# New order tables for four engines in a two-part encoder layer on one core

## The chip, the cores and the metric

The kernel runs on one core of a Trainium2 chip. A core has five engines that run side by side, each through its own list of instructions, strictly in the order of that list: TensorE (PE in the profile; its weight loads are shown apart as PEld), ScalarE (ACT), VectorE (DVE), GpSimd (POOL) and SyncE (SP), which issues the DMAs. An instruction starts when the one before it on its engine is out of the way and when the semaphores that it waits for have been raised by other engines or by DMAs. The metric is the device time of one execution in microseconds, the median of several runs.

## The reference, cut to what matters

One layer of an encoder for 1024 prompt rows and 64 sample rows, all in float32, model width 1024, hidden width 4096:

```python
z = x @ w_in                           # q,k,v of 6 FoX heads and 6 stick-breaking heads, u,v of the SGU
o_fox = softmax(q k^T/8 + c_t - c_s, causal) @ v      # c = cumsum(log f)
o_sb  = stick_breaking(q k^T/8, strictly causal) @ v  # one scan along the keys
o_sgu = gelu(u) * (tril(w_s) @ layer_norm(gelu(v)) + b_s)   # chunks of 128 rows
x1 = layer_norm(ALPHA * x + rms_norm_per_head(concat(o_fox, o_sgu, o_sb)) * g_mix @ w_out)
h  = square(relu(x1 @ w_up))
y  = layer_norm(ALPHA * x1 + h @ w_down)
```

The outputs are `y` for both groups of rows, and the new rows of keys, values, log gates and normalised `v`.

## The kernel before

**Products.** Every float32 operand of a large product is split in a high part, rounded to the type that PE reads (`hi`, written by ACT with a copy), and a low part (`lo = src - hi`, written by DVE or POOL in `lo_sub`, line 303). One product is three passes: high by high, high by low, low by high (`PASSES`). The two MLP products are done as seven block products in place of eight (Strassen's scheme in Winograd's form). PE has 8,827 matmuls.

**Stages.** The times are places in the span of the profile of before. (1) To about 520 us: the input projection (`kv_stage`, `q_stage`, `tok_mm`, line 583) is interleaved with the attention units (scores line 783, transposes line 831, values lines 841 to 844, softmax and stick-breaking rows on ACT, DVE and POOL). (2) 520 to 640 us: `mix`, the output projection (line 461) with its layer norm. (3) 640 to 990 us: the up product in 16 passes `p` of 256 hidden columns; each pass has two chains (`Chain`, s = 0 of 288 rows and s = 1 of 256 rows) of seven products (`product`, line 1536), written to the PSUM banks zA to zD. (4) 990 to 1332 us: the down product (`Down`, line 2001) into A, B and D. (5) After that the last rows' layer norm and their stores.

**The up stage, which the prediction follows in most detail.** For each pass `prep` loads two blocks of `w_up` (tile `wr`, line 1726). ACT and POOL split three blocks of them (tile `wa`, lines 1474 and 303). `w_sums` then forms four sums in place on DVE (lines 1483, 1484, 1486, 1487); ACT writes their high parts (tile `ws`, line 1757) and DVE their low parts (`ws`, line 303). A chain's results leave the banks by ACT (`sn<-zA`, line 1547) and DVE (lines 1550 to 1556). Then DVE does squared relu (line 1568) and four sums (lines 1577 to 1580) on tile `hh`, and SP stores them (lines 1581 to 1585). The first pass (p = 0) uses rows `y` and `h` of the mixer's pool in place of `hh`; the pool of all later passes lies in the same memory, so the first tiles of p = 1 must wait for what still reads the old rows.

**The order.** The Python code above is traced in one program order. After it, at the end of `_build` (lines 2356 to 2368), each engine's instructions are put in an order that is written out, by a planner, in the table `ORDER[engine]`. A table is a row of words `n+k`: take the instruction at place `k` of those that are left, n times (n is 1 and k is 0 where they are not written). Each instruction is made to follow the one taken before it. So a table is a permutation of the program order, and nothing else: it adds, removes and resizes no instruction. Given the permutation of before and the trace, in which the instructions stand in that order, each word of a new table names one instruction of the trace. The places, counts and distances "by the tables" in the prediction are read out in this way. Which buffer of a rotating pool a tile gets is decided by the build, after this order.

Of the kernel before, what the change touches and what calls it, by code (L numbers as in the profile page):

```python
# [50 lines left out]
+4 2 2+2 4 2+23 +25 4+23 12 4+12 2+32 +11 2+31 6 +5 +24 2+5 +51 2 +20 2+51 7+3 2+13 3 +39 +36 8 +10 2 +25 +51  # L51
2+25 6 +46 +2 4 +38 +40 2+14 +36 +65 2+36 +63 +14 4 +58 4 4+6 +79 1 +22 +48 5 +43 17 +53 +26 +52 +53 +82 3+52
2+26 +8 8 2+17 1 8+16 4 4+12 12 +10 18 7+2 +11 1 +10 +11 +10 8+1 1 +1 3 +24 4+27 3+24 32 8+2 1 +1 8 8+1 8+9
2+1 +3 2+6 +3 +1 +2 7+3 +1 8+2 +1 +8 38+1 8+3 2+5 +22 6+5 1 5+15 3 2+12 +14 1 +11 +12 14+11 3+54 +11 5+53
16+58 2+3 2+7 3 4+9 +4 2 4+10 2+2 4+14 2 +6 20+31 +18 1 3+5 1 3+13 +17 +21 +6 2 +14 2 +12 +2 3+13 +2 +10 3+2 2
+6 +5 3 4+7 1 +1 2 +13 1 +12 2+2 4+31 2 2+9 +8 8 +18 7+19 11+2 2+7 +17 +2 7+16 +24 3+2 +15 +2 1 +18 1 +12 +4
+21 +11 +14 2+12 +7 1 2+15 +20 6+9 +3 +5 1 4+11 +2 +5 1 +8 +1 1 2+6 7+12 2+6 +10 8+17 2+2 +19 +8 3+18 +4 +2
2+38 2+3 1 +35 +1 2+34 2+1 2+2 2 2+6 7+26 2+6 3+8 1 2+7 +30 +18 11+7 +25 1 +4 +39 +23 3+4 +13 +19 2+4 2+160
+11 +4 +10 2+31 2+4 3 2+1 1 +6 +146 4+19 +12 +18 +12 2 2+137 +10 3+136 5+138 +4 +137 2+4 +15 1 2+133 1 3+132
+2 +12 4+130 2 +10 +11 +10 +2 3+9 +121 9+122 3+2 2+12 4+2 4+8 +109 2+8 2 3+105 4+14 4 +2 2+96 +2 +8 +94 +2  # L60
3+35 +2 +6 +33 2+6 2+31 +6 2+2 3+4 5+2 +3 2+2 1 2+16 3+1 1 17+62 3+12 1 2+5 1 2+4 2+6 3+51 +6 3+50 2 +48 2+4
+46 2 +44 +2 2+45 4+6 6+2 2 2+36 2+2 2 2+1 2+22 1 2+31 2+6 1 +5 11+27 +5 1 +25 2 2+40 +75 2 2+38 +21 2+41 +21
1 2+66 2+39 6+20 +13 +23 +10 4+18 +12 +31 +17 1 5+47 +29 +46 1 +8 +27 +8 3 +23 2+30 3 +2 2+26 16+30 +13 +29
+13 2 4+26 2+50 6+26 +4 2+45 2+43 4 10+21 +6 4+28 2+2 2+18 +24 +7 +4 3+22 3+29 1 2+41 1 13+27 +4 +26 +13 2
3+26 +11 +25 +2 2+22 +68 5+21 6+31 +35 +31 1 +9 2 2+51 +27 1 +49 +6 2+30 1 +7 +25 1 2+26 +6 2+25 +6 2+22 4
2+30 +18 2+29 +35 +18 +2 +33 1 +8 +15 +1 +23 2+1 +24 +21 +1 +12 +4 +18 +20 +11 +4 +18 +9 +17 1 +3 +15 1 +6 +12
+11 2 +9 1 +3 +7 5+14 1 2+13 8+18 5+20 +88 +20 +87 +13 2+86 6+19 +23 2+19 3+2 2+3 2+2 +12 2+13 1 +11 1 3+10 4
+32 2 +2 8 2+13 6 +13 2+36 +19 +13 7 2+33 +6 2+32 2 +8 2+23 +10 1 +7 3 4+27 +21 +26 +4 1 +24 +19 1 +7 3+2 +14
+17 +48 2+6 +4 +5 +13 2+27 +10 +26 +4 3+38 +4 3+37 +4 +23 1 +8 +33 +13 1 2+19 +12 3+28 2+2 +10 +17 +15 +10 +14
+10 2+20 +10 +2 2+18 +19 2+18 +24 2+4 2+16 2+20 +9 +4 2+18 2+8 2+6 1 +5 2+8 +5 5+7 1 2+25 +4 +5 4+4 2+8 2+4  # L70
3+21 2+15 +6 +20 3+4 2+15 3+4 3+12 +4 2+7 3+11 2+7 1 2+3 1 +2 +4 2+8 8+40 16+42 +43 2 13+41 2+2 +4 2+38 +4 4+2
+4 1 6+1 1 3+6 4 2+2 2 19+13 2+10 8 5+3 5+20 +3 +6 +3 +17 +5 11+16 2+8 +2 2 9+9 2+2 1 +1 1 8+46 2+9 +15 +43
2+9 3+41 2+13 2+4 +49 +37 +11 3+36 +17 +4 3+16 4+39 1 2+38 3+30 2+22 1 8+27 +21 +8 +20 +44 2 +6 +41 +6 +40 +20
+9 +6 4+2 +33 1 +3 +12 +3 +11 1 10+10 2+17 4+2 2+7 3+6 2+2 3+37 8+6 3+13 2 +27 3+24 2+4 4+22 +4 2 4+6 3+15 +25
9+6 6+2 3+10 +38 1 2+15 2+9 2+13 +3 2+8 +1 +9 2+10 +1 +8 +14 2+1 2+6 1 2+23 1 +8 7+14 3+4 +7 +5 3+4 1 2+9 +7 1
+7 2+12 2+2 +4 +2 5+25 2+9 +23 6+2 +17 +5 2+3 8+2 +6 3+8 1 4+7 +16 3+7 1 +12 +67 2 2+4 1 +37 +61 1 +43 1 2+5
+58 +33 +55 1 +32 8 +24 +28 7 +21 +35 6 9+3 +37 +3 +6 +18 +6 +33 1 +4 1 +30 2+14 1 5+27 5+41 4+17 1 +5 +1 1 +3
1 2+11 2+40 +2 +28 2+10 6+36 +2 +35 +17 4+34 +24 +17 +32 1 +10 +1 +21 2+14 4+1 2+10 +20 2+10 2+1 +8 1 +14 4+22
3+2 +19 +4 2+10 +16 +4 +9 +4 +8 +4 +11 +7 +10 +7 +4 5+6 3+4 4+19 2+4 +6 +4 2+5 +4 +12 1 +11 1 2+10 6+2 +9 8+56
5+58 +2 3+57 +8 +3 +11 +7 1 +6 +8 +50 1 4+49 1 2+48 2+6 +46 +47 1 +9 3 5+42 +2 +5 10+40 2+5 3+2 2 +4 5 2+24 3  # L80
3+6 2 12+17 2+29 +17 +30 +42 +17 2+41 1 +28 5+16 +26 +3 1 +13 +23 2 5+11 5+22 1 3+21 4+19 2 11+17 1 2+58 +7 5
+2 3 +48 1 2+10 +16 2+10 1 +13 +4 2+12 22+37 +18 +28 2+4 3+16 +23 +10 2+22 7+26 +15 +25 +10 4 2+20 +39 2+20
+10 2+6 3+17 6 3+11 +22 +2 2+21 5+10 2+16 3+2 +7 +2 +6 +2 4+9 2 4+7 3+14 +7 4+13 2+22 +24 +25 2+24 1 +23 1 +11
1 +4 1 2+16 1 2+7 5+13 5+23 4+7 1 2+6 1 +9 +19 2+14 +17 1 +18 2 2+33 1 +15 2+13 6+29 2+35 +10 +12 1 +32 2 +5
4+29 +23 +28 +8 +5 3+7 3 +18 +7 1 +6 +12 1 +2 +20 +4 2+9 2+2 1 4+14 1 2+13 8+18 3+20 +13 +1 +4 4 +11 +12 +11
3+23 1 3+22 1 +21 2+1 4+19 3+7 1 9+6 1 4+5 1 8+4 4 2+1 +7 +1 +13 +6 8 +4 2+19 2+4 +17 2+18 +17 2+4 2 2+13 +65
8+27 3+41 +6 +40 2+2 2+4 +12 1 +11 1 +32 2+10 2+30 4+10 +26 3+34 4+18 8+30 1 3+29 +17 4+1 +13 1 2+12 +20 3+28
2 2+26 +4 4+17 2 3+19 1 +6 1 4+12 +5 2 +3 1 6+87 +2 4+25 2+82 4+25 2+88 8+80 +25 +2 +78 +24 +5 +12 3+2 2+5
3+17 4+2 2+63 2+3 +2 3+60 +61 1 3+60 3 10+57 +6 2+56 2 3+4 4 4+2 5 +1 2 7+35 +32 4 2+2 7+28 4 +34 +7 +21 +32
+7 4+21 +29 4+41 2+21 +7 +20 +7 +24 3+35 +19 1 2+18 2 2+29 2 2+19 +13 2+24 2 13+22 1 2+19 5 +5 3+55 4+18 +22  # L90
+6 +49 3+5 3 +15 +42 2+15 +6 2 4+37 2+4 16+35 4+16 +10 +30 2+22 2+28 2+22 4 4+22 3+26 +11 +25 +43 2+6 +9 1 +8
+38 6+20 1 +4 5+18 4 2+23 +14 +20 1 +19 7 8+12 6+19 1 2+18 +1 1 2+16 1 +2 5 6+9 8+15 2+23 +2 +22 +2 2 5+19
8+27 +5 1 2+7 2 3+2 1 8+25 6+31 2+11 2+29 4+36 +11 +5 1 +9 2 2+30 2 2+5 2+26 +5 2+3 14+27 2+10 4+25 +3 2+24 +3
3+27 2+10 +8 4+20 3 15+17 +5 2 3+20 2+14 1 2+17 +45 3+17 +2 5+72 5+12 +36 3+66 +80 2+38 4 +32 +73 2+32 1 +31 4
6+65 3+39 1 2+2 +7 2 2+5 2 3+29 1 2+3 +2 2 +4 +22 +4 2+21 +4 2 4+10 +2 2+9 3+2 3+8 2+6 +12 1 +11 +1 +24 +1 2+9
2+21 +1 1 5+19 2+7 1 6+16 2+6 +14 +15 +14 8+21 1 8+28 5+35 +3 2 +2 1 2+1 +9 2+6 +7 +6 +30 2+2 3+21 +1 2+3 1
7+21 4+34 3+60 1 9+33 +1 +49 2+32 +1 4+46 +31 +1 2+17 +42 2 2+15 1 2+37 4+18 5+33 +53 1 +2 1 +50 +1 1 4+48 +13
+9 3 +43 +9 +42 3 2+6 2+3 +4 +3 1 4+4 2 3+14 4+2 3+10 8 3+2 2 5+3 8+5 3+21 +3 2 2+1 2 2+14 2 3+12 8+27 3 3+3 3
+50 4+3 14+14 +4 +3 3 4+9 3 4+6 2+8 2 +6 7+4 7+5 +4 12+13 21+4 2 +2 +9 7+2 5+3 5+14 3+3 2+100 5+3 +2 2 4+3 26
2+18 +2 1 14+1 +44 +1 8 8+15 3+17 15 5+2 1 +3 1 2+5 7+11 3+9 16+10 +2 2+14 +49 1 2+13 10+46 1 +45 1 +6 2+14  # L100
2+22 +39 +5 +21 1 2+12 3+34 +4 +33 +4 +16 19+31 2+23 +10 4 2+18 +40 8+22 +26 +31 1 3+25 3+1 +7 +2 1 +1 2 2+20
2+18 2+2 8+16 4+23 +2 3+22 +9 5+2 +16 1 +15 2+3 1 +12 +2 2 12+9 5+17 +22 2+17 +2 2+19 +2 4+33 +19 4+2 +14 4+27
+14 +11 2+31 +7 4+12 2+2 +10 2+23 +10 +2 +15 1 +3 +1 +6 2+2 +9 +1 +10 1 3+17 +9 3+29 2+7 4+27 3+14 +3 +13 +6
+2 5+11 +15 +72 +2 2+4 2+2 +10 1 8+12 3+9 5+54 1 2+53 4 +24 4+4 1 +3 2 +23 1 +15 3 +12 +4 +11 +35 +11 4 +30
+32 2+30 +10 +7 3 2+6 3 3+20 1 4+2 8+15 2+7 +23 1 +6 +3 +5 +30 +3 1 +28 +20 +17 2+7 +2 +16 2+6 6+16 2+12 3+14
3+12 4+20 8+28 +6 2+2 4+33 1 +3 +7 +14 +7 +3 1 +5 3+25 +5 +2 +11 +8 +10 1 2+9 +7 +16 +7 4+15 1 4+21 6+25 +27
+6 +2 +5 3+24 +11 +5 +22 3+2 +3 3+18 +16 2+17 +2 2 +13 +16 3 6+10 1 2+1 +7 1 2+6 3 5+3 5+17 +3 +8 6+15 1 +7 +2
2 +4 2 +7 3+3 3 4+1 9 4+11 3 2+1 1 +2 1 2+1 5 4+4 +41 1 2+3 2+6 +36 +3 +5 +3 4+33 1 4+32 1 +2 2 +10 2+27 4+19
10+23 +13 +22 +13 +21 6+10 4 2+6 2 +4 2 +2 5 12+30 14 +16 6 +2 1 2+4 +1 29 +11 1 +13 +16 +10 9 +1 +2 +1 51 2+3
2 2+1 1 4+4 4+8 4+12 12+16 1 2+31 1 4+2 +26 2 +8 +23 16+8 +11 1 +3 +6 1 +2 1 2+5 1 +2 1 +1 3 5+23 3 4+4 2+8  # L110
+33 2+8 1 +30 8+11 1 +10 +20 +21 2 +8 1 +7 1 +14 4+6 2+2 +4 2 2+5 1 +4 3+1 1 12+4 4+8 4+12 3+16 3+21 2 +14 1
# [2280 lines left out]
```

## Time and profile before

| what | us |
|---|---|
| median of 3 runs | 1347.11 (1344.9 to 1347.43) |
| the profiled execution, its own time | 1345.63 |
| its span, first to last instruction | 1343.9 |
| PE busy in the span | 1291.4 |
| DVE, ACT, POOL busy | 1003.0, 724.6, 622.8 |

The span and the profiled execution's own time differ by 1.7 us, which lies outside the instructions. A busy share is a mean over stages with different limits. An idle stretch of an engine is shown with its releaser, the instruction or DMA whose end let the engine go on. The lines themselves stand in the prediction, where they are used.

### The profile page before, as it was taken

How to read it: one execution, taken by the hardware profiler on the slowest of the kernel's cores; microseconds unless marked ns; L12 is line 12 of the kernel's file. 1: busy time of each engine (PE TensorE's matmuls, PEld its weight loads, DVE VectorE, ACT ScalarE, POOL GpSimd, SP SyncE). 2: the span in 40 equal slices, each digit the busy share in tenths (PEclk: the TensorE clock that was granted, in tenths of full speed). 3: DMA queues.
4: the chain of work that ended last, by engine and by line, in shares of the span. 5: the costliest groups of instructions: out<-in, count | busy, mean ns of one | idle time of the engine just before them, and what ended most of it. 6: DMA issues, size and time to landing. Idle time of an engine off the chain costs nothing.

```text
span 1343.9 us, 24250 instructions
## 1 busy us (share of the span) xinstructions
PE 1291.4 (96%) x8827; PEld 1183.2 (88%) x8827; DVE 1003.0 (75%) x1797; ACT 724.6 (54%) x1561; POOL 622.8 (46%) x672
## 2 busy tenths in 40 slices
PE   7999999999999999999899999999999999999996
PEld 7999989999988997878799999999987788778885
DVE  4678666677896588798958686877698777677787
ACT  4467666676665575344422232223266676767675
POOL 2231222367675656856322121222187666565657
PEclk9999999999999999999999999999999999999998
DMA  7445564221313357332244534254567443434343
GB/s 228 115 131 157 173 203 120 81 69 53 101 29 87 90 181 272 118 114 71 80 133 134 170 111 159 92 176 143 178 252 264 143 154 123 155 128 139 125 141 133
DMA packets 158048, 185.64 MB, mean 138 GB/s; under 512 B 27740, under 2 KB 116124, under 8 KB 157928
## 3 DMA queue, kind: packets, MB, share of 16 engines
q1 hardware_dynamic: 155832, 183.01, 42.3%
q8 instruction: 70, 1.15, 0.3%
q10 hardware_dynamic: 2096, 1.07, 0.3%
q14 instruction: 50, 0.41, 0.1%
HBM read 117.65 MB, written 60.10 MB: 132 GB/s over the span
## 4 chain that ended last, share of the span: by engine, by line
PE 63%; DVE 15%; DMA 8%; ACT 6%; issue 4%; POOL 4%; SPq 0%; DVEq 0%; ACTq 0%; POOLq 0%
PE A L2001 8%; PE zA L1536 7%; PE mx L461 6%; PE kvsb L583 5%; PE zD L1536 5%; PE kvfox L583 4%; PE D L2001 3%; PE zC L1536 2%; PE zB L1536 2%; DMA rd<-w_down 2%; PE B L2001 2%; PE Sfox L783 2%; PE qsb L723 2%; PE qfox L723 1%; PE Ssb L783 1%
## 5 line engine op out<-in xcount | busy, mean ns | idle before, releaser
L303 POOL TENSOR_TENSOR wa<-wr,wa 128x512 fp32r<-128x512 f32 x41 | 64.4, 1590 | 238.1 <-ACT wa L1474 238.1
L303 POOL TENSOR_TENSOR wd<-rd,wd 128x512 fp32r<-128x512 f32 x77 | 103.5, 1353 | 116.5 <-ACT wd L1474 91.3
L1536 PE MATMUL zA<-xo,ws 128*128 128x288 f32 (+1 forms) x720 | 113.2, 289 | 8.3 <-ACT sn L1547 8.3
L1536 PE MATMUL zD<-xo,ws 128*128 128x288 f32 (+1 forms) x720 | 116.4, 288 | 3.3 <-DVE hh L1550 2.7
L1547 ACT ACTIVATE sn<-zA 128x256 f32<-128x256 f32 (+1 forms) x80 | 31.0, 392 | 149.7 <-PE zA L1536 109.7
L1536 PEld LDWEIGHTS zA<-xo,ws 128*128 128x128 f32 x720 | 99.4, 190 | 9.6 <-ACT sn L1547 9.5
L461 PE MATMUL mx<-xT,oTb 128*128 128x512 f32 (+1 forms) x416 | 105.3, 402 | 1.4 <-DVE y L468 1.4
L1536 PEld LDWEIGHTS zD<-xo,ws 128*128 128x128 f32 x720 | 99.7, 189 | 4.8 <-DVE hh L1550 3.6
L583 PE MATMUL kvfox<-wkvfox,xT 128*128 128x256 f32 (+3 forms) x624 | 96.0, 293 | 4.3 <-ACT wkvfox L559 2.7
L583 PE MATMUL kvsb<-wkvsb,xT 128*128 128x256 f32 (+1 forms) x624 | 93.1, 288 | 0.0
L461 PEld LDWEIGHTS mx<-xT,oTb 128*128 128x128 f32 (+1 forms) x416 | 75.0, 186 | 18.2 <-ACT xo L1415 1.8
L1474 ACT ACTIVATE wd<-rd 128x512 fp32r<-128x512 f32 x105 | 63.9, 623 | 46.2 <-POOL rd L1668 26.1
L583 PEld LDWEIGHTS kvfox<-wkvfox,xT 128*128 128x128 f32 (+1 forms) x624 | 83.3, 190 | 5.0 <-ACT wkvfox L559 3.1
L2001 PE MATMUL A<-wd,wd 128*128 128x512 f32 x312 | 86.5, 390 | 0.5 <-DVE acc L1968 0.5
L583 PEld LDWEIGHTS kvsb<-wkvsb,xT 128*128 128x128 f32 (+1 forms) x624 | 81.1, 187 | 0.1
L769 POOL TENSOR_TENSOR sgsb<-sgsb,snsb 128x127 f32<-128x127 f32 (+7 forms) x48 | 61.7, 1289 | 37.7 <-DVE snsb L767 27.1
L1668 POOL TENSOR_TENSOR rd<-rd 128x512 f32<-128x512 f32 x56 | 76.5, 1366 | 5.7 <-DVE b L303 2.6
L767 DVE TENSOR_TENSOR_SCAN snsb<-snsb,one 128x256 f32<-128x256 f32 (+7 forms) x48 | 69.9, 1461 | 6.3 <-ACT snsb L766 4.2
L2001 PE MATMUL A<-wd,h4a 128*128 128x512 f32 x240 | 70.0, 392 | 1.4 <-ACT p L2018 0.7
L2001 PEld LDWEIGHTS A<-wd,wd 128*128 128x128 f32 x312 | 58.5, 188 | 13.5 <-DVE acc L1968 0.9
L1536 PE MATMUL zB<-xo,wa 128*128 128x288 f32 (+1 forms) x360 | 66.0, 288 | 0.0
L1536 PE MATMUL zC<-xo,wa 128*128 128x288 f32 (+1 forms) x360 | 62.9, 287 | 0.0
(557 smaller groups left out, 3881.0 us busy)
## 6 DMA issues: line engine op xcount, KB each, us to landing
h_dr<-hh SPq DMA_DIRECT2D x30, 512.0 KB, 3.2
rd<-w_down SPq DMA_DIRECT2D x30, 512.0 KB, 5.0
wr<-w_up SPq DMA_DIRECT2D x13, 1024.0 KB, 5.5
hr<-h_dr SPq DMA_DIRECT2D x31, 384.0 KB, 3.5
h_dr<-hh SPq DMA_DIRECT2D x30, 384.0 KB, 2.9
raw<-w_in SPq DMA_DIRECT2D x44, 256.0 KB, 3.2
wo_dr<-swo SPq DMA_DIRECT2D x32, 256.0 KB, 2.3
xT<-wo_dr SPq DMA_DIRECT2D x8, 1024.0 KB, 7.3
```

The lines of the kernel that those rows point to most:

```text
L303: eng.tensor_tensor(out, src, hi.bitcast(F32), op=ALU.subtract)
L461: nc.tensor.matmul(acc[0:m], oT[:, k, hx, 0:m], wo[k // 4][hw][:, k % 4, cs], start=(i == 0), stop=(i == len(seq) - 1))
L583: nc.tensor.matmul(acc[0:n, c0:c0 + n1 - n0], xT[k // 4][:, k % 4, c:c + n], wt[:, k, hw, n0:n1], start=(i == 0), stop=(i == len(seq) - 1))
L723: nc.tensor.matmul(acc[:, 0:w], wq[:, k, hw, :], xT[k // 4][:, k % 4, c:c + w], start=(i == 0), stop=(i == len(seq) - 1))
L767: nc.vector.tensor_tensor_scan(g[:, 0:n][:, ::-1], g[:, 0:n][:, ::-1], one.broadcast_to([P, n]), 1.0, op0=ALU.mult, op1=ALU.bypass)
L769: nc.gpsimd.tensor_tensor(s[:, 0:n - 1], s[:, 0:n - 1], g[:, 1:n], op=ALU.mult)
L783: nc.tensor.matmul(sps[:, b0 - c0:b0 - c0 + n], qd[:, h, s, half * P:(half + 1) * P], kp[b0 // 256][:, h, 0:n], start=(s == 0), stop=(s == ...
L1474: nc.scalar.activation(hi, raw, AF.Copy)
L1536: nc.tensor.matmul(z, w[:, hw, k], xop(s, bo, hx)[:, k, :], start=(new and k == 0 and j == 0), stop=(k == 3 and j == 2), skip_group_check= ...
L1547: nc.scalar.activation(c, z, AF.Copy)
L1668: eng.tensor_tensor(r[:, o], r[:, x], r[:, y], op=ALU.subtract)
L2001: nc.tensor.matmul(z, h[:, hx, q, o], wset[self.c % 2][q][:, hw, wb], start=((n in (0, 3) or n == 1 and self.c == 0) and q == 0 and j == 0 ...
```

## The change

The text of four tables is new: PE, ACT, DVE and POOL. SP's table is the same word for word. Nothing else in the file differs. The tables before were planned without, the new ones with two things: that a DVE step whose operands all lie in SBUF and a POOL step do not run at the same time, and the buffers of the tiles as the build had given them out.

```diff
 ORDER["PE"] = """
-+4 2 2+2 4 2+23 +25 4+23 12 4+12 2+32 +11 2+31 6 +5 +24 2+5 +51 2 +20 2+51 7+3 2+13 3 +39 +36 8 +10 2 +25 +51
...
+3+4 1 +3 4 +23 +26 2+23 +24 3+23 8 +15 4 +38 +34 +11 2+33 +34 6 2+56 2 2+3 2+24 3+3 +49 3 +44 +17 8 +35 4 +31
...
 ORDER["ACT"] = """
-2 +8 1 +4 +6 +3 2+1 1 2+3 2+4 2+2 +5 +2 +6 +4 2 +7 1 +2 1 +6 1 +3 1 +1 1 +1 1 +3 2+2 1 +6 1 +4 3 +3 +1 1 +4 +2
...
+3 +7 1 2+2 2 +2 2+3 +2 2+3 +2 +5 +2 +1 1 +4 1 +1 +2 +5 3 +2 1 2+2 1 +4 2 2+1 2+5 4 +5 +3 +5 2 +1 +12 +1 +11 +3
...
 ORDER["DVE"] = """
-2+3 2 2+2 2+3 2+1 +4 +6 +4 +1 1 +7 +3 3 +3 +4 1 +1 +2 1 +4 +3 2 +1 +11 +10 7 +5 1 +4 1 +3 1 +19 1 +1 +17 +9
...
+2+3 2 +3 +2 +1 2+2 +1 +4 +1 +5 +3 +1 +7 +3 +1 3 +2 +3 +1 +6 +2 1 +1 +2 1 +1 +11 +10 7 +8 +5 1 +4 1 +3 1 +18 +2
...
 ORDER["POOL"] = """
-+321 +3 1 +1 1 +21 +3 +1 +19 2+1 1 +2 1 +1 1 +2 2 2+1 1 +5 +4 8 +6 2 +2 3+1 2 +2 1 +1 1 +2 +5 +8 +5 1 +4 +1 +4
...
++321 1 +2 +1 1 +21 3+1 3 +1 +14 3 +1 1 +1 2 +4 1 +1 1 +1 1 2+2 2 +6 2 +4 +2 +3 +2 7 +1 +4 +5 2 +4 +5 +4 +2 +3
...
```

Read as permutations, old and new table of an engine have the same number of instructions:

| engine | instructions | at another place than before | mean distance moved, us of the old trace | longest move |
|---|---|---|---|---|
| PE | 8,827 | 7,772 | 0.9 | 10.7 |
| ACT | 1,503 | 1,039 | 1.1 | 9.0 |
| DVE | 1,698 | 1,191 | 1.1 | 9.2 |
| POOL | 658 | 412 | 1.4 | 11.7 |
| SP | 672 | 0 | 0 | 0 |

381 rows, old and new, of the table ORDER are left out of this document.

## The prediction

> **What bounds the kernel now.** I read the page first: busy times, slices, the chain that ended last.
>
> ```profile
> span 1343.9 us, 24250 instructions
> ...
> PE 1291.4 (96%) x8827; PEld 1183.2 (88%) x8827; DVE 1003.0 (75%) x1797; ACT 724.6 (54%) x1561; POOL 622.8 (46%) x672
> ...
> PE   7999999999999999999899999999999999999996
> ...
> PE 63%; DVE 15%; DMA 8%; ACT 6%; issue 4%; POOL 4%; SPq 0%; DVEq 0%; ACTq 0%; POOLq 0%
> ```
>
> PE is the bound: it is busy for 1291.4 of 1343.9 us, and its slices are at nine tenths or more everywhere but at both ends and once in the middle. The change keeps all 8,827 matmuls and every other instruction, so PE's busy time stays, and what can change is its idle time, 1343.9 - 1291.4 = 52.5 us. The chain runs through DVE, DMA, ACT and POOL for a third of the span, mostly in places where PE is fed just in time. The view by windows says where PE is idle.
>
> ```profile
> 0.00:50.00 50.00, 42.85 (x337) 42.09 (x337) 24.47 (x57) 23.70 (x55) 14.33 (x38) 1.00 0.60 180
> ...
> 650.00:700.00 50.00, 44.30 (x336) 43.21 (x335) 35.07 (x58) 15.12 (x29) 8.25 (x7) 0.93 0.33 105
> ...
> 900.00:950.00 50.00, 50.00 (x407) 50.00 (x407) 35.97 (x57) 13.95 (x26) 12.20 (x7) 1.00 0.44 150
> ...
> 1300.00:1344.00 44.00, 32.20 (x143) 26.30 (x141) 32.85 (x76) 26.90 (x45) 30.89 (x36) 0.89 0.40 144
> ```
>
> (Columns: stretch, its length, busy us and count of PE, PEld, DVE, ACT, POOL, PE's clock, DMA share and GB/s.) The last 44 us hold 44.00 - 32.20 = 11.8 us of idleness: behind the last matmul only the last rows' norm and their stores are left. The waits of PE, longest first, give the rest.
>
> ```profile
> PE zA L1536 <- ACT sn L1547: 8.3, 5, 5.2
> PE xtp L539 <- DMA xr<-x_prompt: 4.4, 1, 4.4
> PE kvfox L583 <- ACT wkvfox L559: 2.7, 1, 2.7
> PE zD L1536 <- DVE hh L1550: 2.7, 3, 1.3
> PE pkcsb L900 <- DVE kc_sb L303: 1.7, 1, 1.7
> PE qsb L723 <- DVE gsv L590: 1.6, 1, 1.6
> PE kvfox L583 <- DVE qdfox L734: 1.5, 1, 1.5
> PE mx L461 <- DVE y L468: 1.4, 1, 1.4
> PE Ssb L783 <- ACT snsb L766: 1.3, 3, 0.5
> PE B L2001 <- ACT B L1989: 0.9, 1, 0.9
> ...
> PE A L2001 <- POOL wd L303: 0.2, 1, 0.2
> ```
>
> (Total us, times, longest.) The second and third rows are the start, 4.4 + 2.7 = 7.1 us: by the tables the first nine matmuls stand where they stood and SP's order is the same, so I leave these. Start and end off, 52.5 - 7.1 - 11.8 = **33.6 us of PE idleness can be moved by a new order**, 2.5% of the span. That is the whole room of the change on the good side.
>
> **What the new tables know.** The first thing that they were planned with shows in the trace. Single durations (min/median/max ns):
>
> ```profile
> L1577 DVE TENSOR_TENSOR hh<-hh x29: 409/419/1526, 687.3 to 1004.4; 128x256 f32<-128x256 f32 x29
> L1483 DVE TENSOR_TENSOR wr<-wr x14: 676/689/1780, 682.5 to 950.5; 128x512 f32<-128x512 f32 x14
> L303 POOL TENSOR_TENSOR wa<-wr,wa x41: 1281/1472/2456, 682.9 to 957.0; 128x512 fp32r<-128x512 f32 x41
> L1968 DVE TENSOR_TENSOR acc<-acc,A x73: 673/680/690, 1005.4 to 1325.7; 128x512 f32<-128x512 f32 x73
> ```
>
> The same DVE step on SBUF takes 419 ns or up to 1526; one that reads a PSUM bank (A) never leaves 673 to 690. So a DVE step on SBUF stands still while a POOL step runs, and the other way round (1281 to 2456). A plan that lacks this is up to 1.1 us wrong for one step, enough to explain PE's waits, most of which are under 1 us. Of the Trainium skill, the page "SBUF — State Buffer", section "Who interferes with whom", says the same, and one thing more that speaks against the change: who blocks is settled by which of the two starts first. A table orders each engine for itself, not DVE against POOL, so the plan's winner need not be the chip's; that is the third rival.
>
> **The change part by part.** *Durations and counts:* nothing is added, removed or resized, and no DMA issue changes its place in a queue; cost 0. ACT's steps of one function set are not mixed with the other's by the new table, so no table load is added. *The groups PE waited for.* For each stalled matmul I take, by the tables, how much PE work the new order puts ahead of it, at 50.00/407 = 0.123 us a matmul in the up stage and by the trace's own intervals elsewhere. Work that is ready and stands ahead of a stalled matmul shortens its stall by itself, up to the whole stall.
>
> The largest is in the up stage, where p = 0 hands over to p = 1 (timeline):
>
> ```profile
> 661.81 2.43 DVE L303 TENSOR_TENSOR ws<-y,ws 128x1024 fp32r<-128x1024 f32 x2
> ...
> 667.48 0.42 DVE L1579 TENSOR_TENSOR y<-y 128x256 f32<-128x256 f32 x1
> ...
> 667.93 0.34 SPq L1582 DMA_DIRECT2D h_dr<-y  x1
> ...
> 671.17 0.41 ACT L1547 ACTIVATE sn<-zA 128x288 f32<-128x288 f32 x1 [8.19 <-DMA h_dr<-y]
> ...
> 671.64 1.57 PE L1536 MATMUL zA<-xo,ws 128*128 128x288 f32 x5 [5.16 <-ACT sn L1547]
> ```
>
> PE stands 5.16 us, because ACT cannot empty zA before the store of the old rows has left the memory of `sn`; the store waits for DVE's last sum at 667.48, and that stands behind two `ws` steps. In the new tables the second `ws` step (2.43/2 = 1.2 us) stands behind all eight sums, so the store goes 1.2 us earlier; and 29 more matmuls stand ahead of the stalled one, 29 x 0.123 = 3.6 us. Left of the stall: 5.16 - 1.2 - 3.6 = 0.4 us, a gain of 4.8 us.
>
> That stall also costs clock:
>
> ```profile
> 667.00:672.00 5.00, 0.36 (x1) 0.36 (x2) 3.89 (x10) 0.41 (x1) 0.00 (x0) 0.68 0.55 216
> 672.00:674.00 2.00, 2.00 (x10) 2.00 (x10) 0.00 (x0) 0.00 (x0) 0.00 (x0) 0.50 0.97 250
> 674.00:676.00 2.00, 2.00 (x12) 2.00 (x12) 0.00 (x0) 0.00 (x0) 0.00 (x0) 0.59 1.01 301
> 676.00:678.00 2.00, 2.00 (x17) 2.00 (x16) 0.00 (x0) 0.41 (x1) 0.00 (x0) 1.00 1.10 366
> ```
>
> Up to 676 the clock is at half, and in 4 us PE does 10 + 12 = 22 matmuls where it does 17 in 2 us after it: 12 matmuls short, 12 x 0.123 = 1.5 us. The mean of 0.68 in the first row puts the drop 5 x 0.32/0.5 = 3.2 us before 672, some 2 us after PE ran dry. A stall of 0.4 us doesn't get there; a stall left at 2 us or more would, and would keep the 1.5 us. The skill's page "TensorE: Matmul & The Clock Gate", section "HAM oscillation — how this bites in real kernels", sets that limit at about 3.4 us; by it the same 1.5 us go.
>
> Of the other four zA stalls, 8.3 - 5.2 = 3.1 us, two get work ahead:
>
> ```profile
> 739.04 2.15 PE L1536 MATMUL zA<-xo,ws 128*128 128x256 f32 x15 [0.89 <-ACT sn L1547]
> ...
> 761.17 0.38 PE L1536 MATMUL zA<-xo,ws 128*128 128x256 f32 x1 [0.36 <-ACT sn L1547]
> ```
>
> By the tables 8 and 20 more matmuls stand ahead of these, which covers both, 1.25 us; the other two get none or fewer. The other stalls by their rows in the waits: zD, three of 2.7: +26, -1, +3 matmuls: 1.27 + 0 + 0.39 = 1.7. pkcsb: +6, 0.7 of 1.7. qsb: -1, nothing. kvfox: +8, 0.85 of 1.5. mx: +12 wide ones, all 1.4. B: +6 wide ones, all 0.9. Together 1.25 + 1.7 + 0.7 + 0.85 + 1.4 + 0.9 = 6.8 us. The rows from Ssb to the last one above without B, some 13.6 us in stalls of 0.2 to 1.3 us, come out at 5.7 us in the same way. Of all 50 stalled matmuls 28 get work put ahead, 11 lose some, 11 stand as they stood. **Relief: 4.8 + 1.5 + 6.8 + 5.7 = 18.8 us.**
>
> *What is late next.* Work put ahead of one matmul comes earlier itself; 7,772 matmuls and over a thousand steps each on ACT and DVE have other places, so there are new waits. The trace cannot show them. Below they are bounded by 0, above by as much as the old tables leave, 33.6 us. I take 8 us: some 22 new stalls, near half of the 50 that there are, at 0.37 us each, the mean of the stalls other than the long ones (13.6 us in 37). *The end:* by the tables the same steps follow the last matmul on DVE and POOL, in another mix; 0, give or take one of them, 0.7 us.
>
> Sum against the profiled execution: 1345.63 - 18.8 + 8 = 1334.8. The median of the runs lies 1347.11 - 1345.63 = 1.5 above it, so **1336.3 us**, -0.8%.
>
> **The rivals.** (1) *Fuller relief*: the order is right about the port, so few new waits come: -18.8 and next to nothing back, 1328. For: the tables put work ahead of just the longest stalls, 5.16, 1.3 and 1.4 us, as a plan would that foresees them. Against: steps on SBUF go on varying by 1.1 us, and the order between DVE and POOL stays open. (2) *The waits move*: new ones eat the relief, 18.8 us of them, 1347. For: 50 stalls stand in the old tables, which were planned as well; moves average 1 us, like the waits. This is also the case in which the tables don't do what they say: the port's collisions are as many as before and only sit elsewhere. (3) *Slower, by who starts first*: the place is the up stage, passes from 680 to 960 us.
>
> ```profile
> 860.55 1.36 DVE L1568 SCALAR_TENSOR_TENSOR hh<-hh 128x1152 f32<-128x1152 f32 x1
> ...
> 864.20 0.41 DVE L1554 TENSOR_TENSOR hh<-sn,zC 128x256 f32<-128x256 f32 x1
> ...
> 867.21 1.78 DVE L1483 TENSOR_TENSOR wr<-wr 128x512 f32<-128x512 f32 x1
> ```
>
> In this pass the new table puts the weight sum of L1483 seven places earlier, right where L1568 stood, ahead of the two steps that empty zC and zD (L1554 and the second L1556). It must wait for POOL's `wa` and then for the port; the two steps behind it wait with it, and PE for their banks. If POOL wins the port in each pass, that is 1.78 - 0.69 = 1.1 us a pass (maximum less median of L1483), 14 passes, 15.4 us; on top of the 8 us taken and less the 18.8 us of relief it is 1347.1 + 15.4 + 8 - 18.8 = 1351.7. It decides from the point where more than 10.8 us of it reach PE, 0.77 us a pass. Against it: DVE is busy for 35.97 of 50 us there, which takes up 14 us in 50, and L1483 moves earlier in only six of the passes.
>
> **How the numbers follow.** Forecast (relief with some new waits), 1329 to 1344: 0.52. Fuller relief, under 1329: 0.12. Waits move, 1344.4 to 1349.8: 0.14. Slower by the port, above: 0.22. A difference under 0.2%, 2.7 us, is about what a measurement of this kernel can't tell from none. Faster 0.64, same 0.14, slower 0.22. For 8 in 10 the range runs from 1324, below the fuller relief by 4 of the 33.6 - 17.3 = 16.3 us of stalls that the relief (without its 1.5 us of clock) leaves, to 1353, just over the third rival.
>
> **What would show it.** PE busy as before, 1291, less about 2 for the clock, and a span of about 1333. The wait of zA for `sn` near 671 down from 5.2 to under 1 us, and the clock 1.00 in that window; mx, zD and B waits gone. DVE steps on SBUF still up to 1.5 us long, for the port stays. Start 7.1 and end 11.8 us as before. New rows in PE's waits, each under 1 us, of about 8 us together. I am wrong if these sum to more than 16 us, if the zA wait stays above 2 us and keeps its clock drop, or if zC and zD appear near 865 behind L1483.

## The result, and the profile after

The change is faster: 1332.22 us (1330.35 to 1333.29, 4 runs) against 1347.05 us for before beside it, a ratio of 0.989 (0.988 to 0.991). On another chip it came out at 1328.45 us (1326.48 to 1332.06, 5 runs) against 1346.00, 0.987 (0.984 to 0.990). The forecast was 1336.3 with a range of 1324 to 1353.

All lines of the file below the tables stand 25 further down in after: the zA and zD of line 1536 are those of L1561, `sn` of line 1547 is L1572, the sums of lines 1577 to 1580 are L1602 to L1605. The page of after, profiled in an execution of 1333.29 us:

```profile
span 1331.6 us, 24245 instructions
...
PE 1289.3 (97%) x8827; PEld 1184.4 (89%) x8827; DVE 971.5 (73%) x1797; ACT 722.4 (54%) x1561; POOL 602.4 (45%) x672
...
PE   7999999999999998999999999999999999999996
...
PE 76%; DVE 8%; DMA 7%; ACT 3%; POOL 2%; issue 2%; SPq 1%; DVEq 0%; ACTq 0%; POOLq 0%
```

PE's idle time is 1331.6 - 1289.3 = 42.3 us where it was 52.5, and the chain that ended last runs through PE for 76% of the span where it was 63%. DVE is busy 31.5 us less and POOL 20.4 us less for the same instructions, so their steps on SBUF collide less. Two stretches of the view by windows (columns as before):

```profile
650.00:700.00 50.00, 49.06 (x394) 48.39 (x394) 38.12 (x63) 15.21 (x27) 7.10 (x5) 1.00 0.38 121
800.00:850.00 50.00, 47.34 (x367) 47.12 (x366) 33.60 (x50) 12.53 (x24) 10.53 (x6) 0.97 0.44 144
...
1300.00:1332.00 32.00, 20.00 (x89) 16.15 (x87) 24.71 (x54) 16.38 (x27) 23.59 (x27) 0.85 0.37 136
```

The hole at 671 us is gone, 44.30 busy us have become 49.06 and the clock is 1.00. There is a smaller dip at 800 to 850 instead. The end is what it was: 32.00 - 20.00 = 12.0 us of idleness, of which 0.4 us lie past the end of the span. PE's waits:

```profile
PE zD L1561 <- DVE hh L1575: 6.7, 6, 2.7
PE xtp L564 <- DMA xr<-x_prompt: 4.4, 1, 4.4
PE kvfox L608 <- ACT wkvfox L584: 2.5, 1, 2.5
PE osb L866 <- ACT pthsb L824: 2.1, 4, 0.9
PE op L442 <- DVE oo L434: 1.8, 2, 1.5
PE ofox L866 <- ACT osbfox L879: 1.8, 1, 1.8
...
PE zA L1561 <- ACT sn L1572: 0.5, 1, 0.5
```

The 8.3 us of zA have become 0.5, and the rows of mx, of B, of qsb behind `gsv` and of pkcsb at 1.7 are no longer there. zD has gone up from 2.7 to 6.7, and op, osb and ofox are new near the top. Set beside each other instruction by instruction (a stall here is an idle gap of PE of over 150 ns, away from start and end), the two traces give: 50 old stalls of 31.7 us, of which 27.4 us are gone, and 31 new ones of 17.7 us at other matmuls.

### The profile page after: what moved, and what is told of

It is laid out like the page before. It is cut to its first block, busy times and chain, and to the rows that moved or that the text cites. A ratio compares the mean times of both kernels' runs of the same rounds, so it can differ in the third digit from the quotient of the medians.

```text
span 1331.6 us, 24245 instructions
## 1 busy us (share of the span) xinstructions
PE 1289.3 (97%) x8827; PEld 1184.4 (89%) x8827; DVE 971.5 (73%) x1797; ACT 722.4 (54%) x1561; POOL 602.4 (45%) x672
## 4 chain that ended last, share of the span: by engine, by line
PE 76%; DVE 8%; DMA 7%; ACT 3%; POOL 2%; issue 2%; SPq 1%; DVEq 0%; ACTq 0%; POOLq 0%
PE A L2026 11%; PE zA L1561 8%; PE mx L486 6%; PE zD L1561 6%; PE kvsb L608 5%; PE D L2026 5%; PE kvfox L608 4%; PE zC L1561 3%; PE B L2026 3%; PE zB L1561 2%; PE qsb L748 2%; PE Ssb L808 2%; PE sgu L608 2%; PE Sfox L808 2%; DMA rwo<-w_out 2%
## 5 line engine op out<-in xcount | busy, mean ns | idle before, releaser
L328 POOL TENSOR_TENSOR wa<-wr,wa 128x512 fp32r<-128x512 f32 x41 | 60.9, 1505 | 239.2 <-ACT wa L1499 239.1
L1561 PE MATMUL zD<-xo,ws 128*128 128x256 f32 (+1 forms) x720 | 127.5, 290 | 6.7 <-DVE hh L1575 6.7
L1561 PE MATMUL zA<-xo,ws 128*128 128x288 f32 (+1 forms) x720 | 119.9, 288 | 0.8 <-ACT sn L1572 0.5
L1561 PEld LDWEIGHTS zD<-xo,ws 128*128 128x128 f32 x720 | 105.6, 190 | 8.4 <-DVE hh L1575 8.2
L1561 PEld LDWEIGHTS zA<-xo,ws 128*128 128x128 f32 x720 | 102.1, 188 | 1.7 <-ACT sn L1572 1.3
L608 PE MATMUL kvfox<-wkvfox,xT 128*128 128x256 f32 (+3 forms) x624 | 99.8, 296 | 2.9 <-ACT wkvfox L584 2.5
L608 PE MATMUL kvsb<-wkvsb,xT 128*128 128x256 f32 (+1 forms) x624 | 99.1, 290 | 0.2
L1572 ACT ACTIVATE sn<-zA 128x256 f32<-128x256 f32 (+1 forms) x80 | 30.9, 392 | 116.5 <-PE zA L1561 100.9
L2026 PE MATMUL A<-wd,h4a 128*128 128x512 f32 x240 | 74.5, 391 | 0.7 <-ACT p L2043 0.5
L1561 PE MATMUL zB<-xo,wa 128*128 128x288 f32 (+1 forms) x360 | 74.3, 287 | 0.0
L1561 PE MATMUL zC<-xo,wa 128*128 128x288 f32 (+1 forms) x360 | 73.1, 290 | 0.0
L792 DVE TENSOR_TENSOR_SCAN snsb<-snsb,one 128x128 f32<-128x128 f32 (+7 forms) x48 | 67.3, 1408 | 6.8 <-ACT snsb L791 6.3
```

Source lines behind the costliest of these rows:

```text
L328: eng.tensor_tensor(out, src, hi.bitcast(F32), op=ALU.subtract)
L608: nc.tensor.matmul(acc[0:n, c0:c0 + n1 - n0], xT[k // 4][:, k % 4, c:c + n], wt[:, k, hw, n0:n1], start=(i == 0), stop=(i == len(seq) - 1))
L792: nc.vector.tensor_tensor_scan(g[:, 0:n][:, ::-1], g[:, 0:n][:, ::-1], one.broadcast_to([P, n]), 1.0, op0=ALU.mult, op1=ALU.bypass)
L1561: nc.tensor.matmul(z, w[:, hw, k], xop(s, bo, hx)[:, k, :], start=(new and k == 0 and j == 0), stop=(k == 3 and j == 2), skip_group_check= ...
L1572: nc.scalar.activation(c, z, AF.Copy)
L2026: nc.tensor.matmul(z, h[:, hx, q, o], wset[self.c % 2][q][:, hw, wb], start=((n in (0, 3) or n == 1 and self.c == 0) and q == 0 and j == 0 ...
```

## The experiments

Two theories. **T1, the prediction's:** the gain is at the named stalls, above all at zA near 671 us, and comes from PE work put ahead of them and from the second `ws` step moved back. **T2:** the gain is spread, or comes from something that the tables bring with them but that no table shows, such as the buffers that the build gives out after the order.

An edit of a table is written here with `old` and `new` for the permutation of before and of after and `[a:b]` for places in it; where all four engines' old and new prefixes hold the same instructions, a table can be cut and joined. Such cuts lie at 647.5 us of the old trace (place 4725 of PE, 840 of ACT, 902 of DVE, 412 of POOL) and at 962 us (7143, 1015, 1251, 457). The three pieces are called front, up and down. A median stands beside that of before on the same chip.

**One piece at a time.**

```diff
-PE   = old
+PE   = new[:4725] + old[4725:]              # e1, front; ACT, DVE, POOL in the same way
+PE   = old[:4725] + new[4725:7143] + old[7143:]   # e2, up
+PE   = old[:7143] + new[7143:]              # e3, down
```

> The new tables of order up to 647.5 us of the old trace (the attention, the output projection and the head of the up projection), the old ones from there on; the four tables have a common cut there. Theory A (each stage's stalls are its own, so the stages' gains add): the two traces, set beside each other at the same instructions, differ by 5.3 us at that point, so this kernel is 5.3 us faster than before: 1341.8 us. Theory B (a stage that gets done earlier only waits longer at the next stage's first late operand, because loads and stores between them come when they come): the gain is eaten behind the cut, and less than 2 us of it is left: above 1345.

> The new tables from 647.5 to 962 us only (the up projection), the old ones ahead of and behind it. Theory A (the stages' gains add): 5.0 us faster, 1342.1 us: the 5.16 us stall of zA near 671 and its clock dip (1.5 us) gone, 1.3 us of small new stalls net. Theory C (the prediction's weighing, most of the relief lies at the one stall near 671): 6.3 us faster or more, 1340.8. Theory B: under 2 us.

> The new tables from 962 us on (the down projection), the old ones before. Theory A: 2.0 us faster, 1345.0 us; with the two runs above the three gains sum to 12.3 us, close to the whole change's 14.8. Theory B: no change, since the down projection's stalls are set by its loads: 1347.

Measured, against 1347.48: e1 1328.64 us, ratio 0.986 (0.984 to 0.988); e2 1342.17, 0.997 (0.995 to 0.998); e3 1348.86, 1.001 (1.000 to 1.002). Theory A has e2's size right and the rest wrong, C is wrong, and B is right for e3 (no change, though no run shows its reason, the loads) and wrong for the other two: the front alone gains 18.8 us, as much as the whole change, so nothing is left that the 5.3 us of the up piece could be added to, and the down piece gains nothing. In e1 the 5.16 us stall at 671 is gone although every instruction there stands in its old order. One row shows why, ScalarE's copy that empties zA (timeline: start, us, engine, line, in brackets the idle time before it and its releaser). The prediction has it for before, 8.19 us behind a store. In e1:

```profile
657.34 0.41 ACT L1544 ACTIVATE sn<-zA 128x288 f32<-128x288 f32 x1 [2.34 <-PE zA L1533]
```

VectorE's steps before it stand 7.98 us earlier than in before, all by the same amount; this copy stands 13.8 us earlier. It waits for zA alone and not for the store. The builds say what is different: the tile `sn` of the second pass lies at the same address in both, but under it lay `y7` in before, one of the rows that the first pass uses for its `hh`, and `y6` in e1 and after, which no one reads any more by then. The seven buffers of these rows rotate, and the new front order made them rotate differently: 577 of 2,150 tiles have another place in e1 (266 in SBUF, 311 in PSUM).

e2 shows the other way to the same end. There `sn` lies over `y7` as in before, and the copy still starts right behind the landing of the store at 673.02 us (its row names VectorE's last sum of `h`, which ended at 673.06), yet the matmul that stood for 5.16 us in before has no idle time ahead of it:

```profile
673.12 0.41 ACT L1547 ACTIVATE sn<-zA 128x288 f32<-128x288 f32 x1 [7.03 <-DVE h L1579]
```

```profile
673.81 0.29 PE L1536 MATMUL zA<-xo,ws 128*128 128x288 f32 x1
```

Counted from the start of place 4725, the store is issued 17.5 us later in e2 and 20.4 us later in before. So the new up table by itself takes the stall away too, with an earlier store and with matmuls put ahead, as the prediction had it.

**The two moves of the prediction alone.**

```diff
-PE  = old
+PE  = old[:4869] + (29 matmuls of zA, zB, zC, zD that new has ahead of place 4869) + the rest of old
-DVE = old
+DVE = old with place 923 (the second ws step) moved behind place 939 (the last of the eight sums)
```

> The old tables with two moves only, both at the stall of zA near 671 us: VectorE's second ws step goes behind the eight sums of the two passes, and the 29 matmuls that the new table has ahead of the stalled one go ahead of it. The prediction's term for this place: 1.2 us by VectorE's move, 3.6 us by the 29 matmuls, and 1.5 us by the clock, which no longer falls: 6.3 us faster, 1340.8 us, and the half clock from 668.8 to 675.6 gone. Rival (the waits move): the matmuls put ahead leave a hole where they were taken from, and the next step of the same chain is late by as much; then 0 to 3 us faster, 1344 to 1347, with a new stall of zA, zC or zD of over 2 us before 700 us.

Measured: 1345.36 us, ratio 0.999 (0.997 to 1.000), some 2 us. ScalarE's copy and PE behind it:

```profile
673.39 0.41 ACT L1538 ACTIVATE sn<-zA 128x288 f32<-128x288 f32 x1 [7.68 <-DMA h_dr<-y]
```

```profile
673.86 0.40 PE L1527 MATMUL zA<-xo,ws 128*128 128x288 f32 x1 [1.03 <-ACT sn L1538]
...
676.65 1.98 PE L1527 MATMUL zA<-xo,ws 128*128 128x288 f32 x13 [0.50 <-ACT sn L1538]
...
682.39 0.39 PE L1527 MATMUL zA<-xo,ws 128*128 128x256 f32 x1 [0.54 <-ACT sn L1538]
...
689.25 0.50 PE L1527 MATMUL zD<-xo,ws 128*128 128x256 f32 x2 [0.77 <-DVE hh L1541]
```

The 29 matmuls cover what they were said to cover, 5.16 becomes 1.03, and the clock stays at 1.00. VectorE's move brings the store only 0.5 us forward (issued 19.9 us behind place 4725, where it was 20.4), not 1.2. The store still decides when `sn` is free, and the next steps of the same chain are late: 0.50 + 0.54 + 0.77 = 1.8 us of new stalls. About 2.3 of 5.16 us are left as gain. That is the rival's size, 0 to 3 us, though no new stall is over 2 us long.

**The buffer alone.** All four tables old; one tile is declared elsewhere, so the `sn` of this copy lies behind the rows:

```diff
-for tag, n in (("wr", 2048), ("wa", 3072), ("hh1", 2048), ("sn1", 768), ("sn0", 768), ("hh0", 2304), ("ws", 4096),
-               ("hx", 1024)):
+for tag, n in (("wr", 2048), ("wa", 3072), ("hh1", 2048), ("hx", 1024), ("sn1", 768), ("sn0", 768), ("hh0", 2304),
+               ("ws", 4096)):
```

> Before with all its old tables; the one edit is the place of a buffer: the tile hx, used only in the down projection, is declared ahead of sn1, so that the sums' tile sn of the second pass no longer lies on the buffer of y7, which the first pass uses for its hh. Theory D (the 5.16 us stall of zA at 671 us is a buffer wait: ScalarE's copy of zA must not write before the store of hh out of y7 has landed, at 671.1): the stall and its clock dip go without any change of order, 6.7 us faster, 1340.8 us, as they went in the run with the new tables of the front alone. The prediction's theory (the chain of VectorE's steps, the second ws step among them, is late): the stall stays, 1347.5 us.

Measured: 1340.84 us against 1346.30, ratio 0.996 (0.995 to 0.998), 5.5 us. The stall is gone without any new order, as theory D said, and most of its 6.7 us is there. The copy is released by zA:

```profile
668.37 0.41 ACT L1547 ACTIVATE sn<-zA 128x288 f32<-128x288 f32 x1 [2.34 <-PE zA L1536]
```

**The pieces in pairs, and the front's engines apart.** e6 is `new[:7143] + old[7143:]` and e7 `new[:4725] + old[4725:7143] + new[7143:]` for PE, the others in the same way. In e8 ACT, DVE and POOL have the new front, and PE the old one, with 205 instructions moved because the new ones need them earlier. The reverse, PE new and the others near old, was not run.

```diff
-ACT, DVE, POOL = old
+ACT, DVE, POOL = new[:840], new[:902], new[:412] + old behind them
-PE  = old
+PE  = old, 205 instructions earlier
```

> The new tables up to 962 us, the old ones for the down projection. If the gains were independent (front 18.8, up 5.3): 1323.4 us. Theory D (both take away the same stall at 671, so it counts once, and the new up table brings stalls of zD behind hh of its own, 2.8 us net in the trace): 1331.4 us, 2.8 us slower than the front's tables alone.

> The new tables for the front and for the down projection, the old ones for the up projection between them. By the trace of after beside that of the front alone, the new down table is 1.4 us better: 1327.2 us. By the run of the down table alone on the old front (1.4 us slower by the medians): 1330.0 us. Either way faster than after, if the new up table is what costs after its 3.6 us against the front alone.

> In the front (up to 647.5 us) the new order of ScalarE, VectorE and GpSimd, with TensorE's old order but for the instructions that the new ones need earlier; all old behind it. Theory V (the new order of VectorE and GpSimd, with fewer collisions, and the buffers that follow from it carry the front's gain): within 3 us of the front's whole tables, 1328.6 to 1331.6 us. Theory P (TensorE's order carries the 8 us that the front gains in its own stage): only the buffer's 7 us at 671 are left, 1340 us.

Measured, against 1346.30: e6 1329.40 us, ratio 0.988 (0.987 to 0.990); e7 1330.02, 0.988 (0.987 to 0.990); e8 1367.75, 1.016 (1.014 to 1.017). e6 is far from the sum of independent gains (1323.4) and near theory D's 1331.4; e7 bears out the run of the down table alone. With the front new it matters little which up and down tables follow. e8 falls out of both its theories: the new order of the three engines under PE's old one is 21 us slower than before. PE's gaps of over 100 ns in the front sum to 47.1 us, where they are 24.3 in before. They stand at many places:

```profile
PE zA L1524 <- ACT sn L1535: 3.2, 5, 0.9
PE Ssb L771 <- ACT snsb L754: 2.8, 5, 1.0
...
PE ossb L956 <- DVE ptnnsb L291: 2.7, 1, 2.7
...
PE ptfox L819 <- DVE pthfox L291: 2.3, 4, 1.7
...
PE pksb L694 <- DVE kpsb L291: 2.0, 2, 1.2
```

The zA row has no long wait in it, for in e8 `sn` lies on `y2`, free in time as well.

**The buffer put back.** e1 with `sn` over `y7` again:

```diff
-("wr", 2048), ("wa", 3072), ("hh1", 2048), ("sn1", 768), ("sn0", 768), ("hh0", 2304), ...
+("wr", 2048), ("sn1", 768), ("sn0", 768), ("wa", 3072), ("hh1", 2048), ("hh0", 2304), ...
```

> The new tables of the front alone, as in the fastest run so far, with one edit the other way round: the tiles sn1 and sn0 are declared ahead of wa, so that the second pass's sn lies again on the buffer of y7 (in that kernel it lies on y6). Theory D (the stall at 671 is that buffer's): it comes back, at about 658 us, with its clock dip, 6.7 us: 1335.3 us. Rival (the new front also brings the store of y7 earlier than ScalarE needs the buffer, so the place doesn't matter any more): 1328.6 us.

Measured: 1333.88 us, ratio 0.991 (0.988 to 0.993), 5.2 us above e1's 1328.64 (another chip). The stall is back at its old size, PE waits 5.17 us for zA, and ScalarE for the same store:

```profile
662.98 0.41 ACT L1544 ACTIVATE sn<-zA 128x288 f32<-128x288 f32 x1 [8.21 <-DMA h_dr<-y]
```

**A filling by hand, and the change once more.** e10 is e1 with 82 matmuls moved in PE's table; e12 repeats it on e10 with 36. e11 is the change itself.

```diff
-PE = e1
+PE = e1, ahead of each of 13 stalled matmuls 3 to 11 later ones that were ready     # e10
+PE = e10, the same at 9 stalls of e10's own trace                                   # e12
```

> The new tables of the front, and in TensorE's table 82 matmuls moved by hand at 13 stalls of over 0.5 us (11.5 us in all by the trace of the front's kernel): ahead of each stalled matmul go 3 to 11 of the next 60 whose operands were ready by then. If such a filling is gained whole, as the prediction counted the 29 matmuls at 671: 1317.1 us. If half of it comes back as new stalls, as in the run with the two moves at zA: 1323 us. If the waits only move: 1328.6 us.

> The change itself again, on the same chip as the two above. If the 3.6 us between it and the front's tables alone are its new up table, 1332; if they are the spread of the executions (the stage times of the profiles give 307.4 to 309.4 us for both up tables once the buffer is free, and 368.4 to 370.4 for both down tables), 1329 to 1331.

> The kernel with the 82 matmuls moved by hand, and the same filling once more by its own trace: 36 matmuls moved at nine stalls of 0.41 to 1.07 us, 5.1 us in all. By the rate of the first filling (5.7 us of 11.5 by the medians, one half): 1322.9 - 2.6 = 1320.3 us. If what is left is bound by other engines' pace rather than by TensorE's order, the stalls come back whole: 1322.9 us.

Measured: e10 1322.92 us, ratio 0.983 (0.980 to 0.985), and e11 1328.45, both against 1346.00; e12 1323.89 against 1348.41, 0.981 (0.980 to 0.983). The first filling gains 5.5 us on e11 and 5.7 on e1, half of the 11.5 that it fills, as in e4; the second nothing that can be measured. e10 and e12 are the fastest orders found, ahead of both kernels. The 3.6 us that seemed to lie between e1 and after were spread between executions and chips.

**All runs together.** Time from PE's first matmul to place 4725, from there to 7143, and to the end of its last, us of each profiled execution:

| kernel | tables front, up, down | `sn` over | front | up | down |
|---|---|---|---|---|---|
| before | old, old, old | y7 | 643.1 | 314.4 | 370.3 |
| e2 | old, new, old | y7 | 648.2 | 309.6 | 368.5 |
| e3 | old, old, new | y7 | 644.2 | 315.2 | 369.4 |
| e4 | old, old + two moves, old | y7 | 645.8 | 311.4 | 370.2 |
| e5 | old, old, old | no row | 646.1 | 308.2 | 368.5 |
| after | new, new, new | y6 | 637.8 | 309.4 | 368.4 |
| e11 = after | new, new, new | y6 | 630.8 | 307.6 | 369.3 |
| e1 | new, old, old | y6 | 634.8 | 307.4 | 369.1 |
| e6 | new, new, old | y6 | 634.1 | 307.4 | 369.4 |
| e7 | new, old, new | y6 | 636.5 | 307.1 | 370.4 |
| e9 | new, old, old | y7 | 634.7 | 314.0 | 369.2 |
| e8 | mixed, old, old | y2 | 670.4 | 307.9 | 368.9 |
| e10 | new, old, old, filled | y6 | 633.5 | 304.8 | 366.6 |
| e12 | the same, filled twice | y6 | 635.8 | 303.3 | 366.7 |

Means: the front takes 645.5 us with the old tables (five profiles) and 634.8 with the new ones (six): **-10.7**. The up stage takes 314.5 with the old table over `y7` (before, e3, e9), 307.7 with the same table elsewhere (e1, e5, e7, e8) and 308.1 with the new one over `y6` (after, e6, e11): **-6.4**. With the buffer elsewhere the old and the new up table take the same time, so the buffer alone is enough for all of it. The new up table over `y7` gets most of it too (e2, 309.6). Either remedy works by itself; they are for one stall and count once. Down: 369.3 old, 369.4 new, **0**. Together about -17 us, where the two measurements of the change have -14.8 and -17.6. Neither theory holds whole. Most of the gain lies at stalls that the prediction named, 671 and four of the front, as T1 says; but the front gives more than 671, and at 671 the buffer, which no table shows, would have been enough, as T2 says.

In the front, means over the same two groups of profiles, PE's gaps of over 100 ns fall from 26.2 to 19.0 us (start included, 7.2 and 6.9); four stalls make 6.0 of it (places in before's trace): kvfox at 52 us 1.55 to 0.18, qsb at 408 1.61 to 0, pkcsb at 502 1.70 to 0, mx at 582 1.37 to 0. Others grow: ofox at 151 (0.63 to 1.43), pkcsb at 396 (0 to 0.79) and ptsb at 518 (0 to 0.69). The other 3.5 us are in PE's intervals without such a gap, and no run says what made them. Which of PE's order, the other engines' order and the 577 tiles with new places does the front's gain stays open: e8 shows only that the others' new order is no gain under PE's old one.

## Why the prediction was right in the sum, and where it was wrong

**What is bound, and what can move: right.** Start and end stayed (6.9 and 31.6 - 20.0 = 11.6 us), and the gain came out of the 33.6 us of movable idleness, which are 42.3 - 6.9 - 11.6 = 23.8 in after. (The same nine matmuls stand first in both tables, but only the first and the ninth, the two stalled ones, keep their places.) That PE's busy time fell by 2.1 us against the 2 said "for the clock" is luck: the profile of after has 3.4 us at half clock of its own, and e4, with none before the last matmul, is busy for 1291.3 us as before is.

**The stall at 671: the outcome right, the working incomplete.** The wait, its size and its clock dip went as said. The step that failed is the working, "a gain of 4.8 us" from the `ws` step (1.2) and the 29 matmuls (3.6) alone. It took the store behind `sn` as given, though it had read that the copy waits for "the memory of `sn`" and that buffers are given out after the order. In after the copy waits for PE alone:

```profile
659.79 0.41 ACT L1572 ACTIVATE sn<-zA 128x288 f32<-128x288 f32 x1 [4.11 <-PE zA L1561]
```

The buffer without the moves is worth 5.5 us (e5), taking it back costs 5.2 (e9), the two moves without the buffer give 2.1 (e4). The whole new up table without the buffer gives 5.3 (e2), so the size of the term is right and the order could have earned it, but more by VectorE's other steps (the store 3.0 us earlier) than by the `ws` step (0.5 in e4). The 1.5 us of clock at this place came back in one execution: after's profile has 3.4 us at half clock near 824, e11's has none ahead of the last matmul.

**The other named stalls, 6.8 us: under-sized in the front, wrong for zD.** The step counted only PE work put ahead: 0 for qsb, 0.7 for pkcsb, 0.85 for kvfox, 1.4 for mx, 2.95 together. The four lost 6.0 us. Their producers moved too: in e1 the steps of VectorE that released qsb, pkcsb and mx end 0.8, 1.0 and 2.4 us ahead of them, for qsb with one matmul less ahead on PE. zD, with 1.7 us of relief in the sum, got worse by 4.0.

**New stalls, 8 us: too few.** They are 17.7 us, over the 16 that the prediction named as its own refutation, and five of them are over 1 us long where it said "each under 1 us". The net held because the relief was as much too small: 27.4 us of stalls gone against 17.3. So the sum came out near by luck: two terms erred alike by some 10 us, and neither was known.

**The rivals.** The waits did move, by nearly two thirds, but not in full (rival 1347). The second measurement, 1328.45 us, lies where the first rival forecast it, but not for its reason: e11 has 15.1 us of new stalls, not next to none. The third rival's mechanism is in the trace, its price isn't. The weight sum, L1508 in after:

```profile
L1508 DVE TENSOR_TENSOR wr<-wr x14: 678/1590/1832, 670.4 to 940.7; 128x512 f32<-128x512 f32 x14
...
  POOL wa L328: 11.5, 7
```

Its median has gone from 689 to 1590 ns, and VectorE waits 11.5 us for `wa` ahead of it where it waited 5.8. No zC or zD wait followed it near 865. The longest of zD's 6.7 us, at 823, looks like one of this family, but that is not shown. It stands in all four profiles with the new up table (2.51 to 2.67 us) and in none with the old one. VectorE's steps ahead of the stores collide there, the stores are issued late, and zA's copy waits for the buffer of `hh` (timeline of after: VectorE, SP's queue, ScalarE and PE):

```profile
806.66 3.66 DVE L1593 SCALAR_TENSOR_TENSOR hh<-hh 128x1152 f32<-128x1152 f32 x2
810.35 1.40 DVE L1602 TENSOR_TENSOR hh<-hh 128x256 f32<-128x256 f32 x1
811.67 0.68 DVE L1508 TENSOR_TENSOR wr<-wr 128x512 f32<-128x512 f32 x1
```

```profile
816.36 0.52 SPq L1606 DMA_DIRECT2D h_dr<-hh  x1
```

```profile
822.53 0.41 ACT L1572 ACTIVATE hh<-zA 128x288 f32<-128x288 f32 x1 [5.81 <-DMA h_dr<-hh]
```

```profile
823.49 1.72 PE L1561 MATMUL zD<-xo,ws 128*128 128x288 f32 x7 [2.67 <-DVE hh L1575]
```

In the same pass of before, however, VectorE's steps collide by as much, some 2 us over their shortest times in each kernel, and no such stall follows:

```profile
824.17 1.40 DVE L1578 TENSOR_TENSOR hh<-hh 128x256 f32<-128x256 f32 x1
825.49 1.51 DVE L1580 TENSOR_TENSOR hh<-hh 128x256 f32<-128x256 f32 x1
```

```profile
825.64 0.52 SPq L1581 DMA_DIRECT2D h_dr<-hh  x1
...
829.58 0.51 SPq L1582 DMA_DIRECT2D h_dr<-hh  x1
```

What differs is the order: before issues the first of the pass's four stores of `hh` 3.9 us ahead of the others, after issues all four in one row from 816.36. Whether this alone makes the stall was not tried.

**The port.** "DVE steps on SBUF still up to 1.5 us long" holds (L1508 up to 1832 ns), but there are fewer of them. Counted as the time of a step above the lower quartile of its form, where that is over 100 ns, VectorE's SBUF steps lost 84 us in before and 51 in after. In the up and down stages it is 59 in e1 and 38 in e11, and those stages take 676.4 us in e1 and 677.0 in e11: 21 us of collisions less on VectorE, and nothing gained. There, fewer collisions were not what made the time. In the front they fall from 25 us in before to 13 in e1, and e8 has 16 and is 36 us longer than e1. So fewer collisions were not enough there; whether they have a part in the front's gain stays open.

**What was left out.** The prediction valued the stages from one profile. Before's is the shortest front of the five with its tables (643.1 to 648.2), after's the longest of the six with the new ones (630.8 to 637.8); the two together show half of the front's gain.

## What to carry to other kernels

A reordering also re-deals the buffers of rotating pools: before a stall is credited to the new order, look which tile lies under the late one in each build, and try the placement by itself, since one moved declaration here was worth 5.5 us. Two remedies for one stall count once, so test the pieces of a large change one at a time and in pairs. Work put ahead of a stalled matmul gave back about half of its length as new stalls (e4, e10), a second round all of it (e12). In the up and down stages, 21 us less of collisions on an engine that is not the bound gave nothing.

## What the runs showed of the hardware that was not expected

A stall of PE of 2.6 us can cost the clock, and one of the same length need not. In after, behind the 2.67 us stall, and in e2, behind one of 2.62 (windows on PE: busy us and count, clock, DMA share, GB/s):

```profile
822.00:824.00 2.00, 0.51 (x3) 0.98 0.86 226
824.00:826.00 2.00, 2.00 (x11) 0.50 1.06 364
826.00:828.00 2.00, 2.00 (x12) 0.67 0.13 42
```

```profile
832.00:834.00 2.00, 0.00 (x0) 0.99 0.85 272
834.00:836.00 2.00, 1.88 (x8) 0.50 0.96 293
836.00:838.00 2.00, 2.00 (x12) 0.65 0.58 203
```

Both were at half clock for about 3.4 us. In e11 and e6 the same stall was 2.55 and 2.51 us long, and the clock stayed, against the prediction's "a stall left at 2 us or more would" (windows of e11):

```profile
817.00:819.00 2.00, 2.00 (x17) 1.00 0.98 345
819.00:821.00 2.00, 2.00 (x19) 1.00 0.06 22
```

The delay isn't fixed. By the mean clock of such windows it fell 2.3 us after PE ran dry in before, 2.5 in e2 (dry from 834.12 - 2.62), 3.1 in after (dry from 823.49 - 2.67). In e9 PE waits from 658.27 to 663.44, and the clock falls 3 x 0.12/0.5 = 0.7 us before 664, 5.0 us after it ran dry:

```profile
661.00:664.00 3.00, 0.56 (x2) 0.56 (x3) 1.71 (x5) 0.41 (x1) 0.00 (x0) 0.88 0.68 262
```

Length alone does not settle it. The 2.67 us stall of e8 (the ossb row above) kept the clock, and in e12 the clock fell at 514.1, where no stall of PE is longer than 1.14 us. In the clock records of all fourteen traces every change lies a whole multiple of 3.413 us behind the first record. Cut into stretches by these steps, e8's stall lies across an edge and e12's short ones fall into one stretch (e8, then e12):

```profile
462.72:466.13 3.41, 2.58 (x23) 1.00 0.13 38
466.13:469.54 3.41, 1.56 (x13) 1.00 0.13 38
```

```profile
510.72:514.14 3.42, 1.80 (x12) 1.00 0.78 226
514.14:517.55 3.41, 3.41 (x15) 0.50 1.05 404
```

In the stretch that ends with the fall PE sat idle for 2.33 us in before, 2.47 in e2 and 2.67 in after, and for the whole of it in e3 and e9; the stalls of e11 and e6 lie across an edge and leave at most 1.64 us in one. So it counts where a stall lies, and not only how long it is. It is not the whole rule: e12's stretch, with the fall, has PE busy for longer (1.80 us) than e8's without (1.56). What else counts stays open.

The page "TensorE: Matmul & The Clock Gate" of the Trainium skill, section "HAM oscillation — how this bites in real kernels", puts the limit for PE's gaps at about 3.4 us; here gaps of 2.6 us did it, so the measurement decides for this kernel.
